# Two-layer macaron transformer on one core: norms, background products and attention look-ahead reordered in both mixers

## The chip, the cores and the metric

One core of a Trainium2 chip. The time is device microseconds of one execution of the whole program; three runs of the kernel before gave a median of 1093.55 us (1093.55 to 1095.39).

## The reference, cut to what matters

The input is one sequence of 256 tokens with 1024 features, in fp32. Two layers each do feed-forward, mixer, feed-forward, all with a modulated norm and a gated residual:

```
mod = (silu(c) @ ada_w[i] + ada_b[i]).reshape(b, 3, 3, d)          # shift, scale, gate for three blocks
y = rms_norm(x, g) * (1 + scale) + shift                           # before each block
x = x + 0.5 * gate * swiglu(y, ffn_w_in, ffn_w_out)                # blocks 0 and 2 of a layer
x = x + gate * mixer(y)                                            # block 1
```

The mixer of layer 0 ("even") projects y to 1720 columns: a low-rank q (256), a low-rank kv (128) and a rope key (32), each of which gets an rms norm, then q, k and v of a sparse attention (nsa). The low-rank parts go through two up-projections to eight heads (mla), with a norm on each head; the nsa part has eight heads with a compressed, a selected and a windowed branch. Both outputs are concatenated and projected back. The mixer of layer 1 ("odd") projects to 3072 columns and has twelve dilated heads in three groups, joined by their softmax denominators, and four moba heads.

## The kernel before, in words

The 256 tokens are two tiles of 128 (t=0 and t=1). fp32 accuracy in the large products comes from splitting both operands into a rounded part H and a rest L (both fp32r) and adding three matmuls (`mm3`, L204 to L206). Weights are split on the fly: `prep` lets ScalarE (ACT) copy a loaded weight piece to H (L167) and VectorE (DVE) take the difference L (L172). A split piece sits in one of four buffers (`hl`), or in one of four more that a stage opens for pieces of its phase (`open_extra`). `piece(i)` hands a piece to a product, `pop` frees it and prepares the next.

All weights come through one list of load jobs, in order, into eight slots of 1 MB (`pump`). A slot is loaded again when its job is done and all jobs ahead of it are done too; SP issues the loads in that order.

The modulation vectors and gates are computed on DVE beside the rest: slices of `ada_w` come through the same slots, and each slice takes two background steps of two products each (L503). `bg(n)` runs up to n steps, but only those whose slice stands in the job list ahead of the next piece to be prepared. The tuples PT, PD, PC, PB, PA (even mixer) and QT to QA (odd mixer) say how many steps each call may run: PT in the tail of feed-forward 0, PD and PC in the t=0 and t=1 loops of the first projection, PB in the second projection, PA in the attention's iterations. Each call is one tick. When a vector is complete its end is put into `fins` with a due tick: for a norm vector a small matmul and three DVE operations (L551 to L559); for a half gate `finA` (ACT copy L580, DVE difference L581) and `finB` (two matmuls L589, ACT copy L590).

The even mixer goes: first projection (columns 0 to 800) of t=0, then of t=1, in eight steps each; second projection (`proj1`) in eight steps of both tiles; norms of the low-rank parts into `cqn` (L1296 to L1307); transposes into cT and T4; q up-projection (L1348), kv up-projection (L1383), compression (L1415); transposes of q and k (`turn`, L1428); the attention in 16 units (eight mla, eight nsa) and 19 iterations. An iteration runs, on PE, the output product of two units (`s3`), transposes of the probabilities (`turns`) and scores of a later unit (`s0`, with dummy matmuls that `keep_warm` adds); on DVE the scaling of the probabilities and the logits of a later unit; on ACT the exponentials (L1062) and copies (L1100); then `fill`, which runs the compressed branch, background steps and the first parts of the output projection (EF, OF). The odd mixer has the same shape with 8 units and 11 iterations, four of them joint over three branches.

Touched are `open_extra`, `prep`, the job order (EVA, EVO), `gate_steps`, `norm_steps` by FBN, the tuples, `bg_flush`, `attention`, `OutProj.end`, `even` and `odd`.

Of the kernel before, what the change touches and what calls it, by code (L numbers as in the profile page):

```python
# [36 lines left out]
def kernel(  # L37
# [89 lines left out]
    def open_extra(pool, n, ph, w=1024):  # L127
        extra.update(pool=pool, n=n, phase=ph, w=w)
# [204 lines left out]
    EVA = ((0, 1), (0, 2), (0, 3), (1, 0), (1, 1))  # L333
    EVC = (((0, 0, 416), (416, 928, 384)), ((0, 416, 512), (512, 1312, 408)))
    ev_ada = list(plan_ada["ev"])
    for h in range(2):
        m = (800, 920)[h]
        phase[0] = ("ev", -1)[h]
        for kh in range(4):
            add_job(("evi", h, kh), [(  # L340
                lambda t, m=m, d=d, n=n: t[:, 0:2 * m].rearrange("p (k c) -> p k c", k=2)[:, :, d:d + n],
                AP(ev_w_in, kh * 256 * 1720 + c, [[1720, 128], [128 * 1720, 2], [1, n]])) for d, c, n in EVC[h]])
            for k in range(2):
                add_piece(("evi", h, kh), lambda t, k=k, m=m: t[:, m * k:m * k + m], ident_dst, 128, m, k == 1)
            if (h, kh) in EVA:
                ada_slot(*ev_ada.pop(0))
# [21 lines left out]
    EVO = ((0, 1), (1, 1))  # L368
# [194 lines left out]
    def gate_steps(n, q):  # L563
        st = []
        i, b = divmod(n, 3)
        s = 6 * b + q

        def begin():
            st.append(small.tile([128, 512], F32, tag="ada", name="ada", bufs=3))
            G.memset(st[0], 0.0)  # L570
            G.dma_start(st[0][0:1, :], AP(ada_b, i * 9 * D + s * 512, [[512, 1], [1, 512]]))

        def part(jh, js):
            products(st[0], slot4(("ada", i, s, jh)), cact[:, 4 * jh:4 * jh + 4], js, False)
# [40 lines left out]
    FBN = 0, 4, 12, 5, 5, 5  # L615
# [3 lines left out]
    OF = {7: ((0, 0),), 8: ((0, 1),), 9: ((0, 2),)}  # L619
    FBG = 5  # L620
# [53 lines left out]
    def bg_flush():  # L674
        while bgq:
            bg_next()
        due(True)
# [344 lines left out]
    def attention(ap, units, stile, lag, fill, warm):  # L1022
# [106 lines left out]
        s0(0)  # L1129
        s0(1)  # L1130
        logits(0)
        for i in range(n + lag + 1):
            if i >= 2 + lag and (i - lag) % 2 == 0:
                s3(i - 1 - lag)
            if lag == 2 and 2 <= i < n + 2:
# [7 lines left out]
            if lag == 1 and 1 <= i <= n:  # L1143
                turns(i - 1)
            if lag == 1 and i + 2 < n:
                s0(i + 2)
            if i < n:
                exps(i)
            s4()
            if lag <= i < n + lag:  # L1150
                out_of(i - lag)
            settle()
            fill(i)

    class OutProj:
# [27 lines left out]
        def end(self):  # L1183
# [3 lines left out]
            for t in range(2):  # L1187
# [5 lines left out]
                for q in range(2):  # L1193
                    for j in range(QM):
# [18 lines left out]
    def even(blk):  # L1213
# [17 lines left out]
        with tc.tile_pool(name="hlev", bufs=4) as ph:  # L1231
            open_extra(ph, 4, ("ev",), 800)
            heads()
            keep_warm(pa[0][0], WKB[0])
            for k in range(8):
# [3 lines left out]
                if k == TRE:  # L1239
                    piece(7)  # L1240
                    blk.tr(1)
            for k in range(8):
                mm(pa, 0, 1, k, *piece(0))
                pop()
                bg(PC[k])
            close_extra()
        with tc.tile_pool(name="ev", bufs=1) as ep:
# [37 lines left out]
            proj1(0, 2)  # L1285

            c32 = ((0, 256, 256), (256, 384, 128), (384, 416, 32))
# [3 lines left out]
            jk = xtile()  # L1291
            ss = small.tile([128, 2, 3], F32, tag="mss", name="mss")
            rr = small.tile([128, 2, 3], F32, tag="mrr", name="mrr")
            for t in range(2):
                for q, (c0, c1, m) in enumerate(c32):
                    A.activation(jk[:, 0:c1 - c0], pa[t][0][:, c0:c1], AF.Square, accum_out=ss[:, t, q:q + 1])  # L1296
# [24 lines left out]
            for t in range(2):  # L1321
# [4 lines left out]
                V.tensor_copy(T4[0:64, :, 128 * t:128 * t + 128], pv[0:64])  # L1326
                if t == 0:
                    V.tensor_copy(T4[64:128, :, 0:127], pv[64:128, :, 1:128])
                else:
                    V.tensor_copy(T4[64:128, :, 127:255], pv[64:128])  # L1330
# [10 lines left out]
            proj1(4, 6)  # L1341
# [35 lines left out]
            proj1(6, 8)  # L1377
# [11 lines left out]
            for t in range(2):  # L1389
                vw = pb[t][1][:, 0:384].rearrange("p (a c) -> p a c", c=128)  # L1390
                V.tensor_copy(kn[t][:, 1], vw[:, 1])
# [32 lines left out]
            def turn(src, dst, sc, t):  # L1424
                for hh in range(2):
                    ps = acc()
                    for j in range(4):
                        T.transpose(ps[0:96, 128 * j:128 * j + 128], src[:, 4 * hh + j, :], ident)  # L1428
                    scaled_evac(dst[:, 4 * hh:4 * hh + 4, 128 * t:128 * t + 128],
                                ps[0:96, :].rearrange("p (h c) -> p h c", h=4), vec[3][0:96, sc:sc + 1])  # L1430
# [19 lines left out]
            V.tensor_copy(hh, ph[:, 0:256])  # L1450
# [5 lines left out]
            with tc.tile_pool(name="ev2", bufs=1) as e2:  # L1456
# [14 lines left out]
                def nsaT(t):  # L1471
# [4 lines left out]
                    scaled_evac(qT[:, :, tsl], ps.rearrange("p (a c) -> p a c", a=4), gq["n"])  # L1476
# [3 lines left out]
                    scaled_evac(kT[:, :, tsl], ps[:, 0:256].rearrange("p (a c) -> p a c", a=2), gk["n"])  # L1480
# [16 lines left out]
                def c1():  # L1497
# [6 lines left out]
                    V.tensor_copy(cc, pc[0:30, 0:128].rearrange("p (v c) -> p v c", v=2))  # L1504
# [50 lines left out]
                def c8():  # L1555
                    V.tensor_copy(PcT, hold["p"][:, 0:256])
# [3 lines left out]
                def fill(i):  # L1560
# [8 lines left out]
                    if i >= 12:  # L1569
# [37 lines left out]
                bg_flush()  # L1607
# [3 lines left out]
    def odd(blk):  # L1611
# [9 lines left out]
        with tc.tile_pool(name="hlod", bufs=4) as ph:  # L1621
            open_extra(ph, 4, ("od",))
# [14 lines left out]
        with tc.tile_pool(name="od", bufs=1) as op_:  # L1637
# [74 lines left out]
            with tc.tile_pool(name="od2", bufs=1) as o2:  # L1712
# [28 lines left out]
                bg_flush()  # L1741
# [249 lines left out]
```

## Time and profile before

| | us |
|---|---|
| median of 3 runs | 1093.55 |
| profiled execution, its own time | 1094.18 |
| its span, first to last instruction | 1092.4 |
| TensorE busy | 1038.4 |
| VectorE busy | 827.3 |
| ScalarE busy | 532.5 |
| mean granted TensorE clock, share of full | 0.989 |

PE is TensorE, DVE VectorE, ACT ScalarE, POOL GpSimd, SP the engine that issues the loads. Starts are microseconds from the span's start. By the timeline the even mixer's first projection starts behind the transposes at 232, its second at 257.5, its attention at 307.5, its output projection ends at 383.7; the odd mixer's first projection starts behind 770, its attention at 846.3, and its output projection ends at 892.9.

### The profile page before, as it was taken

What the parts mean: (1) busy time and instruction counts of PE and PEld (TensorE: products, weight loads), DVE (VectorE), ACT (ScalarE), POOL (GpSimd) and SP (SyncE); (2) the same over time, 40 slices, a digit from 0 to 9 for tenths busy, and PEclk for the clock granted to TensorE, in tenths of its full rate; (3) what the DMA queues carried; (4) which work ended last, traced back from release to release, by engine and by line L of the source; (5) the groups of instructions that cost most, each with busy time, mean ns of one, the idle gap of its engine ahead of it and who ended that gap; (6) DMA issues with size and microseconds to landing.
All of it is one profiled execution on the core that took longest, in us unless ns stands there. A gap on an engine that the chain in (4) does not pass through costs nothing.

```text
span 1092.4 us, 13983 instructions
## 1 busy us (share of the span) xinstructions
PE 1038.4 (95%) x4983; PEld 837.6 (77%) x4983; DVE 827.3 (76%) x1430; ACT 532.5 (49%) x913; POOL 45.9 (4%) x93
## 2 busy tenths in 40 slices
PE   5899999997889989999999999999999899999998
PEld 5578778876676768888887888888688677888886
DVE  5779867769889689988658998854879868566643
ACT  3444433644258675444446544433645756444441
POOL 3000010002500000000000000000000000000000
PEclk9999999999889999999999999999999999999999
DMA  9999998837690448998853999883288517666401
GB/s 334 320 361 332 325 348 233 286 126 234 240 255 15 154 154 296 365 354 271 283 173 123 308 360 340 289 282 117 77 270 232 163 45 263 226 230 201 155 1 39
DMA packets 169818, 250.77 MB, mean 230 GB/s; under 512 B 10741, under 2 KB 111559, under 8 KB 169748
## 3 DMA queue, kind: packets, MB, share of 16 engines
q1 hardware_dynamic: 166736, 248.35, 69.5%
q0 software_dynamic: 2576, 1.39, 0.9%
q8 instruction: 39, 0.64, 0.2%
q14 instruction: 31, 0.25, 0.1%
q10 hardware_dynamic: 436, 0.13, 0.0%
HBM read 247.59 MB, written 2.23 MB: 229 GB/s over the span
## 4 chain that ended last, share of the span: by engine, by line
PE 76%; DVE 13%; ACT 4%; DMA 4%; issue 2%; POOL 0%; SPq 0%; ACTq 0%; DVEq 0%
PE wps L204 12%; PE wps L206 12%; PE wps L205 12%; PE acc L204 11%; PE acc L206 11%; PE acc L205 11%; DVE L L172 3%; DMA slot<-in_ffn_w_in_dram 2%; DVE ada L503 2%; DMA slot<-in_ada_w_dram 1%; ACT xn L1062 1%; ACT H L167 1%; PE wps L888 1%; DVE xn L1049 1%; PE acc L888 1%
## 5 line engine op out<-in xcount | busy, mean ns | idle before, releaser
L172 DVE TENSOR_TENSOR L<-slot,H 128x1024 fp32r<-128x1024 f32 (+4 forms) x316 | 376.4, 1200 | 128.3 <-ACT H L167 123.4
L167 ACT ACTIVATE H<-slot 128x1024 fp32r<-128x1024 f32 (+4 forms) x316 | 325.6, 1040 | 276.0 <-PE wps L206 137.4
L205 PE MATMUL wps<-L,y 128*128 128x512 f32 (+1 forms) x448 | 174.4, 389 | 5.6 <-DVE L L172 4.7
L204 PE MATMUL wps<-H,y 128*128 128x512 f32 (+1 forms) x448 | 177.3, 396 | 1.7 <-ACT y L1835 1.6
L206 PE MATMUL wps<-H,y 128*128 128x512 f32 (+1 forms) x448 | 173.7, 388 | 0.0
L204 PE MATMUL acc<-H,y 128*128 128x512 f32 (+2 forms) x416 | 162.5, 391 | 3.5 <-ACT y L722 1.6
L205 PE MATMUL acc<-L,y 128*128 128x512 f32 (+2 forms) x416 | 159.6, 384 | 4.0 <-DVE L L172 4.0
L206 PE MATMUL acc<-H,y 128*128 128x512 f32 (+2 forms) x416 | 159.7, 384 | 0.1
L503 DVE SCALAR_TENSOR_TENSOR ada<-slot,c,ada 128x512 f32<-128x512 f32 x155 | 116.2, 750 | 2.9
L205 PEld LDWEIGHTS wps<-L,y 128*128 128x128 f32 x448 | 84.9, 190 | 25.0 <-DVE L L172 9.6
L204 PEld LDWEIGHTS wps<-H,y 128*128 128x128 f32 x448 | 84.9, 190 | 19.4 <-ACT y L1835 2.0
L206 PEld LDWEIGHTS wps<-H,y 128*128 128x128 f32 x448 | 84.7, 189 | 17.4 <-DVE y L728 0.4
L205 PEld LDWEIGHTS acc<-L,y 128*128 128x128 f32 x416 | 78.2, 188 | 19.4 <-DVE L L172 5.9
L204 PEld LDWEIGHTS acc<-H,y 128*128 128x128 f32 x416 | 78.2, 188 | 18.2 <-ACT y L722 1.8
L206 PEld LDWEIGHTS acc<-H,y 128*128 128x128 f32 x416 | 78.1, 188 | 15.7 <-DVE y L728 0.9
L503 DVE SCALAR_TENSOR_TENSOR ada<-slot,cact,ada 128x512 f32<-128x512 f32 x96 | 72.1, 751 | 5.5 <-DMA slot<-in_ada_w_dram 3.6
L204 PE MATMUL acc<-H,gT 128*128 128x512 f32 (+1 forms) x176 | 71.3, 405 | 1.0 <-DVE g L876 1.0
L204 PE MATMUL wps<-H,gT 128*128 128x512 f32 (+1 forms) x176 | 71.2, 404 | 0.0
L206 PE MATMUL acc<-H,gT 128*128 128x512 f32 (+1 forms) x176 | 69.3, 394 | 0.0
L205 PE MATMUL acc<-L,gT 128*128 128x512 f32 (+1 forms) x176 | 69.2, 393 | 0.0
L206 PE MATMUL wps<-H,gT 128*128 128x512 f32 (+1 forms) x176 | 69.1, 393 | 0.0
L205 PE MATMUL wps<-L,gT 128*128 128x512 f32 (+1 forms) x176 | 69.0, 392 | 0.0
(352 smaller groups left out, 1230.9 us busy)
## 6 DMA issues: line engine op xcount, KB each, us to landing
slot<-in_ffn_w_in_dram SPq DMA_DIRECT2D x160, 512.0 KB, 6.7
slot<-in_ffn_w_out_dram SPq DMA_DIRECT2D x40, 1024.0 KB, 7.5
slot<-in_ada_w_dram SPq DMA_DIRECT2D x160, 256.0 KB, 5.6
slot<-in_ada_w_dram SPq DMA_DIRECT2D x24, 1024.0 KB, 8.2
slot<-in_od_w_in_dram SPq DMA_DIRECT2D x12, 1024.0 KB, 5.3
slot<-in_ada_w_dram SPq DMA_DIRECT2D x16, 512.0 KB, 9.5
slot<-in_ffn_w_in_dram SPq DMA_DIRECT2D x16, 384.0 KB, 4.3
slot<-in_nsa_cmp_w_dram SPq DMA_DIRECT2D x4, 1024.0 KB, 9.0
```

The lines of the kernel that those rows point to most:

```text
L167: A.activation(hv, w, AF.Copy)
L172: eng.tensor_tensor(lv, w, hv.bitcast(F32), op=OP.subtract)
L204: T.matmul(o, lhsT=sh, rhs=wh, start=start, stop=False)
L205: T.matmul(o, lhsT=sh, rhs=wl, start=False, stop=False)
L206: T.matmul(o, lhsT=sl, rhs=wh, start=False, stop=stop)
L503: V.scalar_tensor_tensor(a, w[:, j], c[:, j:j + 1], a, op0=OP.mult, op1=OP.add)
L888: T.transpose(ps[0:mm, 256 * ft + 128 * t:256 * ft + 128 * t + 128], st[u, t][:, 128 * ft:128 * ft + mm], ident)
L1049: V.tensor_tensor_reduce(out=s[b][:, 128:384], in0=ps[:, 128:384], in1=M[:, 0:256], scale=-1.0, scalar=3e38, op0=OP.add, op1=OP.min, accum ...
L1062: A.activation(s[b][:, c0:c1], s[b][:, c0:c1], AF.Exp, scale=-1.0, bias=nm[:, b, q:q + 1], accum_out=den[:, b, q:q + 1])
```

## The change

The load order of the even mixer puts two modulation slices ahead of the first projection's weights, one behind the sixth and one behind the eighth of its loads, and the four gate slices two and two around the output weights. `prep` fills the four common buffers first and the extra ones after them in the mixers. A half gate's `finB` is put on the list only when `finA` has run, three ticks later. The tuples have new quotas. At the end of the attention `bg_end` runs what is left but only one end; `OutProj.end` runs the others ahead of the second half of the first tile's last products. `attention` issues scores three units and logits two units ahead of the iteration (two and one before). In the even mixer the squares of tile 0 are taken inside the t=1 loop, the norms of the low-rank parts are issued ahead of the second projection, whose eight steps now stand 2, 1, 2, 3 between the norms, the transposes, the q and the kv up-projection (they stood 2, 2, 2, 2); and some fifteen copies and scalings out of PSUM go to ScalarE in place of VectorE.

```diff
-        if extra["live"] < extra["n"] and ph in extra["phase"]:
+        if npre[0] >= cap[0]:
+            return False
+        here = extra["live"] < extra["n"] and ph in extra["phase"]
+        if len(ready) - extra["live"] < HLN and not (here and not extra["last"]):
+            pool = hl
+        elif here:
             pool = extra["pool"]
             extra["live"] += 1
-        elif len(ready) - extra["live"] < HLN:
-            pool = hl
...
-    EVA = ((0, 1), (0, 2), (0, 3), (1, 0), (1, 1))
+    EVA = ((1, 1), (1, 3))
     ev_ada = list(plan_ada["ev"])
+    for _ in range(2):
+        ada_slot(*ev_ada.pop(0))
...
-    for a in ev_ada:
-        ada_slot(*a)
     for j in range(4):
+        if j % 2 == 0:
+            for _ in range(2):
+                ada_slot(*ev_ada.pop(0))
         add_job(("evo", j), [(
...
-    EVO = ((0, 1), (1, 1))
+    EVO = ((0, 1), (1, 1), (2, 1), (3, 1))
...
             owed.append(lambda: V.tensor_tensor(st[2], st[0], st[1].bitcast(F32), op=OP.subtract))
+            fins.insert(0, (tick[0] + FBG, finB))
...
-            [(2, finA), (FBG, finB)]
+            [(2, finA)]
...
-    FBN = 0, 4, 12, 5, 5, 5
+    FBN = 0, 4, 5, 5, 5, 5
-    OF = {7: ((0, 0),), 8: ((0, 1),), 9: ((0, 2),)}
-    FBG = 5
+    OF = {6: ((0, 0),), 7: ((0, 1),), 9: ((0, 2),)}
+    FBG = 3
+    AH = 2
-    PA = 1, 1, 0, 1, 0, 1, 1, 1, 1, 1, 1, 1, 1, 1, 1, 1, 1, 2, 1, 0
-    PT = 2, 1, 0, 1, 0, 0, 0, 0
+    PA = 1, 1, 0, 1, 0, 0, 0, 0, 0, 0, 0, 0, 0, 0, 0, 1, 1, 1, 1, 0
+    PT = 0, 0, 1, 1, 0, 0, 0, 0
-    PC = 1, 1, 1, 1, 2, 1, 1, 1
-    PB = 1, 1, 1, 2, 1, 1, 0, 0
+    PC = 0, 1, 0, 1, 0, 1, 1, 0
+    PB = 1, 1, 0, 0, 0, 0, 1, 0
-    QC = 0, 0, 0, 0, 0, 0, 0, 0
+    QC = 0, 1, 0, 1, 0, 0, 0, 0
...
-    def bg_flush():
+    def bg_end():
         while bgq:
             bg_next()
-        due(True)
+        if fins:
+            fins.pop(0)[1]()
...
-        s0(0)
-        s0(1)
-        logits(0)
+        for i in range(AH):
+            s0(i)
+            if i == 0:
+                continue
+            logits(i - 1)
+        s0(AH)
+        logits(AH - 1)
         for i in range(n + lag + 1):
...
-            if lag == 2 and i + 2 < n:
-                s0(i + 2)
+            if i + AH + 1 < n:
+                s0(i + AH + 1)
             if 1 <= i <= n:
                 scale(i - 1)
-            if i + 1 < n:
-                logits(i + 1)
+            if i + AH < n:
+                logits(i + AH)
...
                 for q in range(2):
+                    if q:
+                        due(True)
...
+            cap[0] = npre[0] + 16
...
+                if k == 3:
+                    for q, (c0, c1, m) in enumerate(c32):
+                        A.activation(jk[:, 0:c1 - c0], pa[0][0][:, c0:c1], AF.Square, accum_out=ss[:, 0, q:q + 1])
...
-            proj1(0, 2)
...
-                V.tensor_copy(kn[t][:, 0], pa[t][1][:, 256:384])
+                A.activation(kn[t][:, 0], pa[t][1][:, 256:384], AF.Copy)
                 for q, (c0, c1, _) in enumerate(c32):
-                    V.tensor_scalar(cqn[t][:, c0:c1], pa[t][0][:, c0:c1], rr[:, t, q:q + 1], None, op0=OP.mult)
+                    if t:
+                        A.activation(cqn[t][:, c0:c1], pa[t][0][:, c0:c1], AF.Copy, scale=rr[:, t, q:q + 1])
+                    else:
+                        V.tensor_scalar(cqn[t][:, c0:c1], pa[t][0][:, c0:c1], rr[:, t, q:q + 1], None, op0=OP.mult)
...
+            proj1(0, 2)
             bank[0] = acc
-            proj1(2, 4)
+            proj1(2, 3)
...
-            proj1(4, 6)
+            proj1(3, 5)
...
-            proj1(6, 8)
+            proj1(5, 8)
...
+                    if (t, hh) == (0, 1):
+                        V.tensor_scalar(dst4, src4, g, None, op0=OP.mult)
+                    else:
+                        A.activation(dst4, src4, AF.Identity, scale=g)
...
+                    if i == 11:
+                        cap[0] = 1 << 30
-                    if i >= 12:
+                    if i >= 11:
                         prep(True)
```

## Rows read from the trace of the kernel before

**Rows 1.** The page's first part: busy us, share of the span, instructions.

```profile
PE 1038.4 (95%) x4983; PEld 837.6 (77%) x4983; DVE 827.3 (76%) x1430; ACT 532.5 (49%) x913; POOL 45.9 (4%) x93
```

**Rows 2.** Waits of PE by line: releaser; us in total, times, longest.

```profile
PE acc L1318 <- DVE cqn L1307: 6.5, 2, 6.0
...
PE wps L589 <- DVE ahl L581: 3.0, 1, 3.0
...
PE wps L1090 <- ACT PT L1100: 2.6, 1, 2.6
...
PE acc L1383 <- issue: 1.3, 1, 1.3
...
PE acc L1415 <- POOL qf L1281: 0.9, 1, 0.9
```

**Rows 3.** Windows: stretch, busy us (instructions) by engine, PE clock, DMA share, GB/s.

```profile
270.00:280.00 10.00, 5.85 (x23) 5.19 (x24) 6.81 (x23) 0.95 (x2) 4.51 (x11) 0.66 1.08 360
...
280.00:290.00 10.00, 9.90 (x40) 7.01 (x39) 9.00 (x13) 1.97 (x4) 3.00 (x4) 1.00 0.54 188
...
310.00:320.00 10.00, 6.64 (x38) 5.77 (x37) 9.39 (x36) 4.38 (x16) 2.07 (x4) 0.83 1.09 327
...
320.00:330.00 10.00, 9.35 (x62) 7.73 (x60) 7.01 (x31) 6.06 (x22) 0.00 (x0) 0.83 0.96 202
...
330.00:340.00 10.00, 10.00 (x74) 7.06 (x74) 9.54 (x45) 7.16 (x26) 0.00 (x0) 1.00 0.01 4
...
380.00:390.00 10.00, 7.37 (x35) 5.38 (x34) 7.52 (x17) 8.75 (x14) 0.00 (x0) 1.00 0.00 0
```

**Rows 4.** Timeline of PE: start us, us, engine, line, tile; idle before it.

```profile
273.69 0.45 PE L1318 MATMUL acc<-cp,cqn 128*128 128x128 f32 x1 [6.00 <-DVE cqn L1307]
...
277.29 0.78 PE L204 MATMUL wps<-H,y 128*128 128x512 f32 x1
...
279.45 0.39 PE L204 MATMUL wps<-H,y 128*128 128x512 f32 x1
```

**Rows 5.** Timeline of DVE in the same stretch.

```profile
259.56 6.49 DVE L503 SCALAR_TENSOR_TENSOR ada<-slot,c,ada 128x512 f32<-128x512 f32 x8
...
265.97 3.11 DVE L503 SCALAR_TENSOR_TENSOR ada<-slot,cact,ada 128x512 f32<-128x512 f32 x4
...
271.05 0.30 DVE L488 TENSOR_SCALAR mss<-mss 128x2 f32<-128x2 f32 x3
...
274.07 0.89 DVE L1307 TENSOR_SCALAR cqn<-acc,mrr 128x256 f32<-128x256 f32 x3
```

**Rows 6.** Timeline of DVE and PE in the first attention iterations.

```profile
316.39 0.68 DVE L581 TENSOR_TENSOR ahl<-ada,ahl 128x512 fp32r<-128x512 f32 x1
...
318.78 1.06 PE L1036 MATMUL wps<-yb,yb 96*128 96x256 f32 x2
...
323.54 0.60 PE L1036 MATMUL wps<-yb,yb 96*128 96x256 f32 x2
```

**Rows 7.** Timeline of DVE and PE around the even attention's end.

```profile
363.58 3.49 DVE L172 TENSOR_TENSOR L<-slot,H 128x1024 fp32r<-128x1024 f32 x3
...
371.88 0.42 DVE L841 TENSOR_TENSOR yb<-acc,yb 128x256 fp32r<-128x256 f32 x1 [4.81 <-ACT yb L840]
...
372.22 1.22 DVE L172 TENSOR_TENSOR L<-slot,H 128x1024 fp32r<-128x1024 f32 x1
...
372.61 0.39 PE L206 MATMUL wps<-H,oT 128*128 128x512 f32 x1
```

**Rows 8.** Timeline of ACT and PE in the odd attention.

```profile
856.75 0.40 ACT L1062 ACTIVATE xn<-xn,nj 128x128 f32<-128x128 f32 x1 [2.57 <-DVE nj L1053]
...
873.68 0.90 PE L1090 MATMUL wps<-cp,xn 128*128 128x128 f32 x3 [2.56 <-ACT PT L1100]
...
874.23 0.78 PE L204 MATMUL acc<-H,oTo 128*128 128x512 f32 x1
```

**Rows 9.** Timeline of SP's DMA queue behind the even projections.

```profile
304.66 9.60 SPq L101 DMA_DIRECT2D slot<-in_ffn_w_in_dram  x6
```

More of the change, by code (lines that the diff above doesn't have):

```diff
@@ L125, in add_piece, with open_extra @@
         pieces.append((name, src, dst, rows, cols, last, phase[0]))
-    def open_extra(pool, n, ph, w=1024):
-        extra.update(pool=pool, n=n, phase=ph, w=w)
+    cap = [1 << 30]
+    def open_extra(pool, n, ph, w=1024, last=False):
+        extra.update(pool=pool, n=n, phase=ph, w=w, last=last)
     def close_extra():
@@ L1134, in attention @@
                 s3(i - 1 - lag)
-            if lag == 2 and 2 <= i < n + 2:
+            if 2 <= i < n + 2:
                 turns(i - 2)
-            if lag == 2 and i + 2 < n:
-                s0(i + 2)
+            if i + AH + 1 < n:
+                s0(i + AH + 1)
             if 1 <= i <= n:
                 scale(i - 1)
-            if i + 1 < n:
-                logits(i + 1)
[L1143 to L1146, printed above, removed]
+            if i + AH < n:
+                logits(i + AH)
             if i < n:
@@ L1231, in even @@
         with tc.tile_pool(name="hlev", bufs=4) as ph:
-            open_extra(ph, 4, ("ev",), 800)
+            open_extra(ph, 4, ("ev",), 800, True)
+            cap[0] = npre[0] + 16
             heads()
@@ L1241, in even @@
                     blk.tr(1)
+            jk = xtile()
+            ss = small.tile([128, 2, 3], F32, tag="mss", name="mss")
+            c32 = ((0, 256, 256), (256, 384, 128), (384, 416, 32))
             for k in range(8):
@@ L1284, in even @@
             bank[0] = None
-            proj1(0, 2)
-            c32 = ((0, 256, 256), (256, 384, 128), (384, 416, 32))
             cqn = [e1.tile([128, 416], F32, name=f"cqn{t}") for t in range(2)]
@@ L1290, in even @@
             qn = ep.tile([128, 2, 4, 2, 64], F32, name="qn")
-            jk = xtile()
-            ss = small.tile([128, 2, 3], F32, tag="mss", name="mss")
             rr = small.tile([128, 2, 3], F32, tag="mrr", name="mrr")
-            for t in range(2):
-                for q, (c0, c1, m) in enumerate(c32):
-                    A.activation(jk[:, 0:c1 - c0], pa[t][0][:, c0:c1], AF.Square, accum_out=ss[:, t, q:q + 1])
+            for q, (c0, c1, m) in enumerate(c32):
+                A.activation(jk[:, 0:c1 - c0], pa[1][0][:, c0:c1], AF.Square, accum_out=ss[:, 1, q:q + 1])
             kcd = xtile()[:, 0:1024].rearrange("p (t a b c) -> p t a b c", t=2, a=4, b=2)
@@ L1325, in even @@
                 pv = ps.rearrange("p (a c) -> p a c", a=4)
-                V.tensor_copy(T4[0:64, :, 128 * t:128 * t + 128], pv[0:64])
+                A.activation(T4[0:64, :, 128 * t:128 * t + 128], pv[0:64], AF.Copy)
                 if t == 0:
-                    V.tensor_copy(T4[64:128, :, 0:127], pv[64:128, :, 1:128])
+                    A.activation(T4[64:128, :, 0:127], pv[64:128, :, 1:128], AF.Copy)
                 else:
-                    V.tensor_copy(T4[64:128, :, 127:255], pv[64:128])
+                    A.activation(T4[64:128, :, 127:255], pv[64:128], AF.Copy)
             AA = xtile()[:, 0:1024].rearrange("p (v i a) -> p v i a", v=2, i=16)
@@ L1390, in even @@
                 vw = pb[t][1][:, 0:384].rearrange("p (a c) -> p a c", c=128)
-                V.tensor_copy(kn[t][:, 1], vw[:, 1])
+                A.activation(kn[t][:, 1], vw[:, 1], AF.Copy)
                 jk = xtile()[:, 0:768]
@@ L1428, in turn @@
                         T.transpose(ps[0:96, 128 * j:128 * j + 128], src[:, 4 * hh + j, :], ident)
-                    scaled_evac(dst[:, 4 * hh:4 * hh + 4, 128 * t:128 * t + 128],
-                                ps[0:96, :].rearrange("p (h c) -> p h c", h=4), vec[3][0:96, sc:sc + 1])
+                    src4, dst4 = ps[0:96, :].rearrange("p (h c) -> p h c", h=4), dst[:, 4 * hh:4 * hh + 4, 128 * t:128 * t + 128]
+                    g = vec[3][0:96, sc:sc + 1]
+                    if (t, hh) == (0, 1):
+                        V.tensor_scalar(dst4, src4, g, None, op0=OP.mult)
+                    else:
+                        A.activation(dst4, src4, AF.Identity, scale=g)
             kf = []
@@ L1449, in even @@
             hh = PcT
-            V.tensor_copy(hh, ph[:, 0:256])
+            A.activation(hh, ph[:, 0:256], AF.Copy)
             V.tensor_scalar(gt, gt, 1.0, None, op0=OP.add)
@@ L1475, in nsaT @@
                         T.transpose(ps[:, 128 * p:128 * p + 128], qn[:, t, p].rearrange("q g c -> q (g c)"), ident)
-                    scaled_evac(qT[:, :, tsl], ps.rearrange("p (a c) -> p a c", a=4), gq["n"])
+                    A.activation(qT[:, :, tsl], ps.rearrange("p (a c) -> p a c", a=4), AF.Identity, scale=gq["n"])
                     ps = acc()
@@ L1479, in nsaT @@
                         T.transpose(ps[:, 128 * b:128 * b + 128], kn[t][:, b], ident)
-                    scaled_evac(kT[:, :, tsl], ps[:, 0:256].rearrange("p (a c) -> p a c", a=2), gk["n"])
+                    A.activation(kT[:, :, tsl], ps[:, 0:256].rearrange("p (a c) -> p a c", a=2), AF.Identity, scale=gk["n"])
                 def fold():
@@ L1503, in c1 @@
                                      start=k == 0, stop=k == 1)
-                    V.tensor_copy(cc, pc[0:30, 0:128].rearrange("p (v c) -> p v c", v=2))
+                    A.activation(cc, pc[0:30, 0:128].rearrange("p (v c) -> p v c", v=2), AF.Copy)
                     A.activation(kcn[:, 0], cc[:, 0], AF.Square, accum_out=sk)
@@ L1555, in c8 @@
                 def c8():
-                    V.tensor_copy(PcT, hold["p"][:, 0:256])
+                    A.activation(PcT, hold["p"][:, 0:256], AF.Copy)
                 chain = [c0, c1, c2, c3, c4, c5, c6, c7, c8]
@@ L1606, in even @@
                 attention(e2, units + [mk2(p, b) for p in range(4) for b in range(2)], ring, 2, fill, WKE)
-                bg_flush()
+                bg_end()
                 return proj_out.end()
@@ L1621, in odd @@
         with tc.tile_pool(name="hlod", bufs=4) as ph:
-            open_extra(ph, 4, ("od",))
+            open_extra(ph, 4, ("od",), 1024, True)
             heads()
@@ L1740, in odd @@
                 attention(o2, units, ring, 2, fill, WKO)
-                bg_flush()
+                bg_end()
             return proj_out.end()
```

## The prediction

> **What bounds the kernel now.** Start with the busy shares [rows 1]: TensorE (PE) is busy 1038.4 of 1092.4 us. No edit removes matmuls, so all that can be won is the 54 us in which PE stands, and the time it runs at the lower clock. The waits of PE come next [rows 2]: five of the longest lie in the two mixers. 6.5 us is the transposes of the normed latents waiting for VectorE (DVE, L1307); 3.0 is a gate matmul behind L581; 2.6 is a transpose behind ScalarE's copy L1100; 1.3 and 0.9 are L1383 and L1415. The rest are block seams and feed-forward stages the diff leaves alone. The windows [rows 3] show what such a wait costs beside itself: in 270 to 280 us the granted clock averages 0.66 (of its two levels, 2.4 and 1.2 GHz, the lower for about two thirds of the stretch), while ScalarE has 0.95 us of work and DVE 6.81.
>
> Why does PE wait at 267.7? Read the two engines side by side [rows 4, 5]. PE has finished four of the eight steps of the second projection and needs cqn. DVE executes in order and has twelve modulation products ahead of the norm: eight from 259.56 to 265.97 and four to 268.99. The mean starts at 271.05, cqn follows at 273.07 and 274.07. So the norm is late because of what stands ahead of it on DVE, not for want of data.
>
> Durations below come from the profiled execution, 1094.18 us (span 1092.4 and 1.78 around it). The median shown, 1093.55, is 0.63 below; I take that off at the end.
>
> **The change part by part.** A background step is two products, 1.5 us of DVE (four products take 3.11) [rows 5]. The second set of modulation vectors takes eight steps, the gate of the first mixer's output eight.
>
> *Steps that move.* A step runs only where its call has a quota and its slice stands ahead of the next weight piece in the load queue. Walking the new order through that rule: the first two slices are now ahead of the first projection, so two steps run in the tail of feed-forward 0 and one at the end of the t=0 loop; the t=1 loop runs three, at k=1, 3 and 5; the quotas at k=6 and at steps 0 and 1 of the second projection find a slice that still stands behind unprepared pieces, so nothing; one runs at step 6. That is seven. Three follow in the first four attention iterations, one each in iterations 15 to 18, two in the flush behind. In the old order ten ran up to the norm, four later in the projection, two in the attention. So seven steps, 10 us of DVE, leave the stretch ahead of the norm, and six land at the attention's end.
>
> *Norms ahead of the second projection.* Three of six squares run inside the t=1 loop. With DVE free by about 257.5, the norm chain (3.8 us by the rows from 271.05 to the end of cqn at 274.9) plus some 2.2 us of squares and copies on ScalarE ends near 263, while PE does three projection steps, 2.5 us each by its four in 10.1 us, until 265.1. I cost the norm at nothing: these three steps hide it, with some 2 us to spare. This takes away the 6.00 and 0.47 us of waiting and the lower clock behind it: from 273.69 to 279.45 fourteen transposes and six matmuls take about 2.2 us more than at the full clock (0.78 us for the 512-column matmul at 277.29, 0.39 at 279.45) [rows 4]. Together 8.7 us.
>
> *Three projection steps behind the q up-projection instead of two.* They give DVE 7.5 us for the q norm, which took 5 us plus the 1.3 us that L1383 waited [rows 2]: 1.3 goes. Of the 0.9 at L1415 I take half, as it may rest on ScalarE's copies of v as well. The price: six of eight evacuations of qf and kf now queue on ScalarE, so that the first scores come about 0.5 us later. The other copies moved there, of 0.3 to 0.7 us, meet an engine with 1.97 us of work in 280 to 290 [rows 3], where DVE has 9.00: nothing. An ACT version of these scalings is not in the trace; bounds: 0.1 us saved each, as the ScalarE twins of L836 are slightly shorter, to 1 us lost in all if they queue. Front of the even mixer: 8.7+1.3+0.5-0.5 = 10.0 us; bounds 6, if one of these waits moves to a copy, and 11.
>
> *Gate in two steps.* The gate's end (copy to fp32r on ScalarE, difference on DVE, matmul) was run in one go in iteration 0; PE reached the matmul and waited 3.04 us for L581, queued behind an hT chain, and then ran below the clock (L1036 x2 1.06 us at 318.78, 0.60 at 323.54) [rows 6]. Now the matmul follows three calls later, and here it leaves the place altogether. But DVE is nearly the bound there: in the three windows from 310 to 340 it idles 4.06 us [rows 3]; three steps instead of two add 1.5, while two evacuations and two small copies sent to ScalarE (2.2, an estimate by the sizes of L581) and two differences that leave (1.36) take off 3.5. Of the 6 us that PE loses I therefore take 2.6; bounds 0 and 6. Scores and logits two units ahead help DVE use the idle time; their order adds no instruction. In the nsa units the score tiles are a ring of nine for ten now live: one write waits for the transposes of the same iteration, which PE has already queued. Nothing, as PE is busy without a gap there; bound 2 us lost.
>
> *The end of the even attention.* Here the change adds a wait. In iteration 18 DVE waits until 371.88 for the last output (L841), having idled since 367.07, then splits a piece (L172, 1.22) [rows 7]. The new order queues behind: step 14 of 16, the first gate difference (0.68, L581 in [rows 6]), steps 15 and 16, another split, the second difference. The first gate matmul stands in PE's queue right behind the product that ends near 372.8; its difference is ready at 371.9+0.3+1.1+1.5+0.6 = 375.4: PE waits 2.6 us, with all of the output projection queued behind. As behind the wait in the odd mixer [rows 8], I add 1.4 for the lower clock. The four gate matmuls themselves, 0.25 each, now stand where PE is the bound: 1.0; the second difference, 0.3. Sum 5.3 lost; bounds 0, if DVE reaches it in time, and 7, if two more splits stand ahead.
>
> [...] The granted clock in 380 to 390 stays at 1.00 though PE is busy only 7.37 us [rows 3], and behind the wait of 2.56 a 512-column matmul takes 0.78 [rows 8]. [...]
>
> *Odd mixer.* ScalarE waits for DVE's logits ahead of every joint exponential (2.57 us at 856.75) while DVE does the scaling and a background step of the unit before; that is what delays L1100 and makes PE wait 2.56 us at 873.68 with slow matmuls behind, to 876.5 [rows 8]. Two units ahead, the logits are there, and all eight background steps of this mixer now run in the projections, where the earlier preparation of two pieces frees DVE 2.5 us. From that wait and 1.4 of clock, 4.0 in all and some small waits beside, I take 3.7, since scaling of a joint unit must still wait for the logits ahead of it on DVE; bounds -1 and 5.
>
> Other moved items at nothing: the cap and the pool order change where pieces lie, not how many; DMA issues on SP are the same number, two slices earlier; the gate's bias load and memset on POOL follow their steps. Sum: -10.0-2.6+5.3-3.7 = -11.0; 1094.18-11.0-0.63 = 1082.6 us.
>
> **Rivals.** (a) No pile-up at the end: the last steps slip into DVE's idle 4.81 us [rows 7] and the early attention gives its 6. Against it: DVE is in order and step 14 is issued behind L841. 5.3-1.0+3.4 = 7.7 better: 1075. (b) A wait takes the place of the one removed: cT or T4 waits for ScalarE, whose queue now has squares, copies and splits ahead, or the early attention stays bound by DVE. Half of the front lost and nothing in the attention: 5+2.6 worse: 1090. For it: DVE was at 9.00 in 280 to 290. Against: ScalarE is nearly idle there. (c) Slower: the eight load slots are freed in order, and slices of the gate now sit in them until iterations 16, 18 and the flush. Feed-forward 1 had three double loads issued from 304.66 [rows 9]; now one is in before iteration 16. Price: six slices of 1 MB at the 360 GB/s of [rows 3] are 2.8 us each, 16.8 us of debt; if none of it hides, 1082.6+16.8 = 1099. It decides when more than four of the six (11 us) fall on PE; against it speaks that DMA moves nothing in 380 to 390 [rows 3], and that the next loads are not wanted before about 390. (d) Everything cancels: 1093.5.
>
> **How the numbers follow.** Forecast 1082.6 (own range 1079 to 1087) 0.56; (a) 0.14; (b) 0.18; (d) 0.04; (c) 0.08. Leaving out the lower half of (a), (d) and (c), about 0.19, the range is 1075.5 to 1090.5. About 0.2% (2.2 us) is what measurements of this kernel can tell: faster 0.88, within 0.04, slower 0.08.
>
> **What would show it.** Right: no wait of PE on cqn, granted clock 1.00 between 265 and 290, attention starting some 10 us earlier; no wait of about 3 us at the first gate matmul in iteration 0, but one of 2 to 3 us at L589 just ahead of the output projection; in the odd mixer joint exponentials back to back and no wait near 2.5 us on L1100. Wrong: a wait of several us at cT, at L1383 or at the first matmuls of feed-forward 1 for slots; or an unchanged length of the odd attention.

## The result, and the profile after

The changed kernel takes 1082.46 us (median of 4, 1079.88 to 1083.83) against 1094.47 for the kernel before on the same chip (4 runs, 1093.55 to 1095.66): a ratio of 0.9887, 95% interval 0.9865 to 0.9909. The forecast was 1082.6. The profiled execution of the changed kernel is its fastest, 1079.88 us, with a span of 1078.1 from the first instruction to the last, 14.3 under the span before. So the parts below add up to 14.3, not to the 12.0 between the medians.

The page of the changed kernel, first part: busy us, share of the span, instructions (as [rows 1]).

```profile
PE 1035.7 (96%) x4983; PEld 835.0 (77%) x4983; DVE 819.0 (76%) x1412; ACT 539.7 (50%) x931; POOL 43.5 (4%) x93
```

PE's busy time is 2.7 us less for the same 4983 instructions; the rest of the 14.3 us is time in which it stood. Its waits by line (as [rows 2]: releaser; us in total, times, longest; the old L1318 is L1339, L589 is L599, L1090 is L1103):

```profile
PE acc L599 <- DVE ahl L590: 2.3, 1, 2.3
PE acc L1103 <- DVE xn L1094: 1.8, 2, 1.2
...
PE acc L1726 <- ACT qTo L847: 1.2, 1, 1.2
PE acc L1133 <- ACT PT L1113: 1.2, 1, 1.2
...
PE acc L1345 <- ACT cT L847: 0.3, 1, 0.3
```

All five waits of [rows 2] are gone from their places. The largest new one, 2.3 us, is the gate matmul's, now at the even attention's end. Windows of the changed kernel (columns as [rows 3]):

```profile
270.00:280.00 10.00, 10.00 (x41) 7.38 (x40) 4.80 (x15) 1.96 (x4) 2.59 (x5) 1.00 0.31 106
310.00:320.00 10.00, 9.33 (x67) 6.69 (x66) 8.74 (x45) 4.15 (x16) 1.01 (x2) 0.83 1.05 304
360.00:370.00 10.00, 10.00 (x38) 8.10 (x37) 7.03 (x12) 3.45 (x8) 0.49 (x1) 0.84 0.88 311
370.00:380.00 10.00, 7.78 (x31) 5.46 (x30) 8.25 (x17) 8.75 (x13) 0.00 (x0) 0.85 0.03 5
380.00:390.00 10.00, 9.31 (x37) 7.28 (x36) 9.62 (x19) 4.29 (x8) 0.00 (x0) 0.81 0.87 295
```

From 270 to 280 PE is busy throughout at the full clock, where it had 5.85 us at 0.66. Behind the new wait, in 360 to 370, the granted clock is low. It is low again from 370 to 390, behind the first waits of the next block; that costs nothing, as the stage lengths below the table show. The front in DVE's and PE's timelines (as [rows 4, 5]):

```profile
255.87 3.21 DVE L512 SCALAR_TENSOR_TENSOR ada<-slot,c,ada 128x512 f32<-128x512 f32 x4
259.00 0.40 DVE L497 TENSOR_SCALAR mss<-mss 128x2 f32<-128x2 f32 x3
...
261.12 0.90 DVE L1327 TENSOR_SCALAR cqn<-acc,mrr 128x256 f32<-128x256 f32 x3
...
264.15 0.82 PE L1339 MATMUL acc<-cp,cqn 128*128 128x128 f32 x6
```

Four products stand just ahead of the norm, not twelve; cqn is done at 262.0, 2.1 us before PE comes to it. The even attention's end (as [rows 7]):

```profile
357.19 1.53 DVE L512 SCALAR_TENSOR_TENSOR ada<-slot,cact,ada 128x512 f32<-128x512 f32 x2
358.63 0.68 DVE L590 TENSOR_TENSOR ahl<-ada,ahl 128x512 fp32r<-128x512 f32 x1
359.23 3.11 DVE L512 SCALAR_TENSOR_TENSOR ada<-slot,cact,ada 128x512 f32<-128x512 f32 x4
...
359.37 0.50 PE L599 MATMUL acc<-ahl,onesr 128*128 128x512 f32 x1 [2.31 <-DVE ahl L590]
...
360.44 0.63 PE L212 MATMUL wps<-H,yb 128*128 128x512 f32 x1
```

To place the time, take the starts of the same rows in PE's timeline of each profiled execution and subtract. A: the even mixer's first transposes to its first scores; B: on to the first product with the compressed values (VB); C: on to the last of these; D: on to the next block's transposes; E: the odd mixer's second transposes to its first scores; F: on to the start of its last output product with v; G: on to the next transposes. In the kernel before, for instance, F and G part here:

```profile
883.16 2.17 PE L1120 MATMUL wps<-PT,vt 128*64 128x256 f32 x16
...
892.90 1.04 PE L703 MATMUL wps<-cp,xn 128*128 128x128 f32 x8
```

| kernel | A | B | C | D | E | F | G |
|---|---|---|---|---|---|---|---|
| before | 75.75 | 39.02 | 22.83 | 14.35 | 63.24 | 36.87 | 9.74 |
| after | 64.27 | 35.23 | 22.81 | 19.55 | 64.37 | 32.30 | 9.74 |
| norm behind (e1) | 66.58 | 35.23 | 22.84 | 18.19 | 64.31 | 32.16 | 9.74 |
| products ahead (e2) | 76.45 | 36.37 | 23.31 | 14.34 | 64.30 | 32.29 | 9.74 |
| gate early (e3) | 64.26 | 35.23 | 24.18 | 15.31 | 64.31 | 32.32 | 9.74 |
| one ahead (e4) | 64.29 | 34.10 | 23.83 | 18.19 | 65.87 | 34.42 | 9.75 |
| odd steps back (e5) | 64.42 | 35.22 | 22.82 | 19.51 | 63.31 | 32.12 | 9.73 |
| gate one go (e6) | 76.63 | 36.37 | 23.29 | 14.35 | 64.33 | 32.17 | 9.74 |
| copies on DVE (e7) | 64.34 | 37.97 | 22.70 | 18.17 | 64.33 | 32.55 | 9.73 |
| steps in idle (e8) | 64.27 | 34.50 | 24.16 | 15.31 | 64.34 | 32.51 | 9.74 |
| norm end late (e9) | 75.34 | 37.11 | 23.30 | 14.34 | 64.34 | 32.40 | 9.74 |
| gate early, odd steps back (e10) | 64.28 | 35.24 | 24.17 | 15.30 | 64.80 | 32.12 | 9.74 |
| all three (e11) | 64.26 | 34.56 | 23.70 | 15.30 | 63.30 | 32.12 | 9.74 |

After minus before: A -11.48, B -3.79, C -0.02, D +5.20, E +1.13, F -4.57, G 0. From D's end to E's start both take some 399.3 us, though the clock is low from 370 to 390 in the changed kernel alone. Another -0.88 lies ahead of the first mixer: its transposes start anywhere from 228.9 to 233.5 us in these profiles, and what sets that was not tested. What is left is 0.1.

### The profile page after: what moved, and what is told of

Read it like the earlier page. It is cut to its first block, busy times and chain, and to the rows that moved or that the text cites. A ratio compares the mean times of both kernels' runs of the same rounds, so it can differ in the third digit from the quotient of the medians.

```text
span 1078.1 us, 13969 instructions
## 1 busy us (share of the span) xinstructions
PE 1035.7 (96%) x4983; PEld 835.0 (77%) x4983; DVE 819.0 (76%) x1412; ACT 539.7 (50%) x931; POOL 43.5 (4%) x93
## 4 chain that ended last, share of the span: by engine, by line
PE 81%; DVE 9%; DMA 4%; ACT 3%; issue 1%; SPq 1%; ACTq 0%; DVEq 0%
PE wps L210 12%; PE wps L212 12%; PE wps L211 12%; PE acc L210 12%; PE acc L212 12%; PE acc L211 12%; DVE L L178 3%; DMA slot<-in_ada_w_dram 2%; DMA slot<-in_ffn_w_in_dram 1%; ACT H L173 1%; SPq L101 1%; PE wps L901 1%; PE acc L901 1%; DMA yb<-scr 1%; PE wps L1133 1%
## 5 line engine op out<-in xcount | busy, mean ns | idle before, releaser
L210 PE MATMUL acc<-H,y 128*128 128x512 f32 (+2 forms) x416 | 164.2, 395 | 4.0 <-ACT y L735 1.6
L212 PE MATMUL acc<-H,y 128*128 128x512 f32 (+2 forms) x416 | 161.6, 388 | 0.1
```

Source lines behind the costliest of these rows:

```text
L210: T.matmul(o, lhsT=sh, rhs=wh, start=start, stop=False)
L212: T.matmul(o, lhsT=sl, rhs=wh, start=False, stop=stop)
```

## The experiments

The kernel before took 1094.37 us beside e1 to e4, 1095.23 beside e5 to e8 and 1094.57 beside e9 to e11. Executions of one kernel scatter by up to 6 us, so the table above, in which stages that an edit leaves alone mostly repeat to 0.2 us, tells more than a median where the edit is small.

**e1: the norm behind two projection steps again.**

```
+            proj1(0, 2)
             cqn = [e1.tile(...) ...]     # squares, mean, scaling
             ...
-            proj1(0, 2)
             bank[0] = acc
```

> The changed kernel with one thing undone: the squares, the mean and the scaling of the latents stand behind steps 0 and 1 of the second projection again, and the moved modulation products stay where the change put them. In the changed kernel cqn is ready at 262.0 us and PE wants it at 264.15, so 2.1 us are spare. Theory A (both halves of the edit were needed): the two splits of steps 0 and 1 stand ahead of the squares on ScalarE, and the second can only start when PE frees its buffer, about 261.7; squares to 263.7, mean and scaling 3 us, cqn at 266.7: PE waits 2.5 us at the latents' transposes and pays some 1.5 us of lower clock behind: 4 us slower, about 1086.5. Rival (the products alone were the cause): the spare time hides the two steps, no wait, 1082.5. Rival (the place alone was the cause): the wait of 6.5 us is back with 2.2 us of clock: 1091.

1084.16 us (ratio 0.9904, 0.9887 to 0.9921). PE's waits show the one that theory A had:

```profile
PE acc L1339 <- DVE cqn L1328: 2.2, 1, 2.2
```

A grows by 2.31 us, the wait alone: the granted clock stays at 1.00 behind it, so theory A's 1.5 us of clock did not come. The norm's place is worth 2.3 us while the products are out of the way. The rivals fall.

**e2: the modulation products ahead of the norm again.**

```
-    EVA = ((1, 1), (1, 3))          # two slices also ahead of the first
+    EVA = ((0, 1), (0, 2), (0, 3), (1, 0), (1, 1))
-    PC = 0, 1, 0, 1, 0, 1, 1, 0     # PT, PB, PA likewise
+    PC = 1, 1, 1, 1, 2, 1, 1, 1
```

> The changed kernel with the old order of the modulation slices in the load queue and the old quotas of the even mixer: some ten steps run ahead of the norm again and two in the attention; the norm keeps its new place. Theory A: at the front DVE gets to the norm at about 265 us, cqn at 268, PE wants it at 264.2: a wait of about 4 us and 2 us of clock, 6 us lost; at the attention's end the wait of 2.3 us on the first gate difference, the lower clock behind it and the late steps go, 5.3 us won: about 1083, the same as the change. Rival (where the norm stands was the cause of the front's gain): nothing lost at the front, 5.3 won at the end: 1077. Rival (the end's 5.3 was not the steps' doing but the seam's): 6 lost, nothing won: 1088.5.

1090.36 us (0.9966, 0.9955 to 0.9978), 7.9 slower than the change. D is 14.34, so the 5.2 us at the end are the late steps' doing, as theory A had it. The front lost twice what it expected, 12.2 us. PE's waits from 255 to 310, three rows of its timeline and two windows:

```profile
PE acc L1336 <- DVE cqn L1324: 4.4, 1, 4.4
PE acc L1342 <- ACT cT L844: 1.7, 1, 1.7
PE acc L1433 <- POOL ada L576: 1.6, 1, 1.6
PE acc L557 <- DVE ada L509: 1.0, 1, 1.0
```

```profile
265.19 1.03 PE L557 MATMUL acc<-cp,ada 128*128 128x4 f32 x8 [1.02 <-DVE ada L509]
...
270.63 1.51 PE L1336 MATMUL acc<-cp,cqn 128*128 128x128 f32 x6 [4.42 <-DVE cqn L1324]
...
294.18 3.60 PE L1401 MATMUL acc<-slot,cT 128*128 128x512 f32 x8
```

```profile
260.00:270.00 10.00, 5.19 (x29) 4.40 (x27) 9.30 (x23) 0.08 (x1) 3.55 (x9) 0.87 1.07 367
270.00:280.00 10.00, 7.68 (x31) 6.75 (x32) 5.04 (x10) 7.26 (x13) 6.83 (x16) 0.62 0.95 314
```

By the starts of the cqn transposes (264.15 in the changed kernel, 270.63 here), 6.6 of the 12.2 come ahead of them: waits of 4.4 and 1.0 us, and the matmuls at L557 themselves, 1.0, which the changed kernel runs in B. The other 5.6 come behind: waits of 1.7 and 1.6 us, and the lower clock (0.62 in 270 to 280). The kv up-projection (L1401), which waited 1.3 us in the kernel before, doesn't wait here.

**e3: two gate steps earlier in the even attention.**

```
-    PA = 1, 1, 0, 1, 0, 0, 0, 0, 0, 0, 0, 0, 0, 0, 0, 1, 1, 1, 1, 0
+    PA = 1, 1, 0, 1, 0, 0, 0, 0, 0, 0, 0, 0, 0, 1, 1, 1, 1, 1, 1, 0
```

> The changed kernel with two quotas more: steps 11 and 12 of the first gate run in attention iterations 13 and 14, so that the last four steps run in 15 to 18 and none is left for the flush. Theory A (the end's price is DVE's queue: 2.3 us of wait, the lower clock of three windows behind it, the relocated matmuls): the first difference is done two iterations earlier, DVE's idle 2.42 us ahead of the last output takes a step in, the wait goes, clock 1.00 from 360 to 400: 4 us won, about 1078.5, with the second difference still in the flush. Rival (DVE at 9.76 of 10 us in 340 to 350 is the bound): the steps delay the outputs by the 3 us they take, and nothing is won: 1082.5 or slower. Rival (the lower clock comes from the block seam): only the wait goes, 2.3 won: 1080.

1078.58 us (0.9855, 0.9840 to 0.9870), the time that theory A had. PE no longer waits at the gate matmul, and the clock stays up behind it:

```profile
350.00:360.00 10.00, 10.00 (x57) 7.77 (x57) 9.56 (x18) 4.82 (x8) 1.01 (x2) 1.00 0.82 265
360.00:370.00 10.00, 10.00 (x46) 8.25 (x45) 7.47 (x17) 5.37 (x10) 0.00 (x0) 1.00 0.84 301
```

It still falls at the next block's start (0.76 in 370 to 380), against theory A's 1.00 up to 400, and again at no cost (399.3 us from D's end to E's start). D falls by 4.24; C, where the two steps now run, grows by 1.37, the share of the first rival. So the trace shows 2.9 us, less than the 3.9 between the medians and theory A's 4. The 0.96 by which D stays above the kernel before are the four gate matmuls.

**e4: scores and logits one unit ahead.**

```
-    AH = 2
+    AH = 1
```

> The changed kernel with scores and logits one unit ahead, as before the change, in both attentions. Theory A (looking two units ahead is what removed ScalarE's waits ahead of the joint exponentials): in the odd attention the wait near 2.5 us on the copy of the transposed probabilities is back with its slow matmuls, 4 us lost; in the even attention 0 to 2 us lost: about 1087. Rival (the eight background steps that left the odd attention did it): the odd attention stays as it is, 1082.5. Rival (the even attention's early part gained its 3.8 us by the look-ahead): another 3.8 lost, 1090.

1082.84 us (0.9891, 0.9873 to 0.9909), not theory A's 1087: no difference that the medians can tell. The trace can. ScalarE's idle times ahead of the four joint exponentials of the odd attention are back, by its timeline:

```profile
842.37 0.40 ACT L1075 ACTIVATE xn<-xn,nj 128x128 f32<-128x128 f32 x1 [0.90 <-DVE nj L1066]
848.55 0.40 ACT L1075 ACTIVATE xn<-xn,nj 128x128 f32<-128x128 f32 x1 [2.57 <-DVE nj L1066]
854.80 0.40 ACT L1075 ACTIVATE xn<-xn,nj 128x128 f32<-128x128 f32 x1 [1.51 <-DVE rd L1090]
862.05 0.40 ACT L1075 ACTIVATE xn<-xn,nj 128x128 f32<-128x128 f32 x1 [2.25 <-DVE nj L1066]
```

The 2.57 is that of [rows 8] to the digit; in the changed kernel only 0.91 and 0.93 are left of the four. F is 2.12 longer, half of what theory A expected. In the even attention two units ahead only trade B (+1.13) for C (-1.02).

**e5: the odd mixer's background steps back among its attention's units.**

```
-    EVO = ((0, 1), (1, 1), (2, 1), (3, 1))      -    QC = 0, 1, 0, 1, 0, 0, 0, 0
+    EVO = ((0, 1), (1, 1))                      +    QC = 0, 0, 0, 0, 0, 0, 0, 0
```

> The changed kernel with the odd mixer's gate slices where they stood before and no steps in the t=1 loop of its projections; the look-ahead of two stays. The background steps run among the odd attention's units again. In the run with scores one unit ahead the odd attention took 34.4 us from its first scores to its last output, against 32.3 in the changed kernel and 37.5 before, so some 3 us should belong to the steps. Theory A: 3 us lost in the odd attention, 1.1 won back in the projections ahead of it: 1084.4. Rival (with two units ahead the steps are covered): the attention keeps 32.3, the projections give 1.1 back: 1081.4.

1080.14 us (0.9878, 0.9859 to 0.9896). F stays at 32.12 and E gives 1.06 back: the rival. Either edit alone shortens F (36.87 to 34.42 with the steps out and one unit ahead, to 32.12 with the steps in and two ahead), and with two ahead the steps' move only costs. (The expectation's 37.5 for the kernel before is 36.9 when F ends where that product starts, as in the other kernels.)

**e6: e2 with the gate's end in one go.**

```
-            fins.insert(0, (tick[0] + FBG, finB))     # in finA
-            [(2, finA)]
+            [(2, finA), (FBG, finB)]                  # FBG = 5
```

> The kernel of the run with the modulation products ahead of the norm again (1090.4), and in it the gate's end in one go as before: copy, difference and matmul in the same call. Theory A (the split in two steps is what removed the wait of 3.04 us in attention iteration 0): the wait is back with slow matmuls behind it, 3.5 us more from the first scores to the first output of the second kind (36.4 to about 39.9): 1094. Rival (the early attention is bound by DVE and the wait only stood for that): no more than 1 us longer: 1091.

1091.30 us (0.9968, 0.9955 to 0.9980), B 36.37 as in e2. The split in two steps is worth nothing, in this kernel with the vectors' end due after 5 calls.

**e7: the evacuations back on DVE.**

```
-                A.activation(T4[0:64, ...], pv[0:64], AF.Copy)       # and kn, cqn, cc, PcT, hh
+                V.tensor_copy(T4[0:64, ...], pv[0:64])
-                    A.activation(qT[:, :, tsl], ..., AF.Identity, scale=gq["n"])   # kT, qf, kf
+                    scaled_evac(qT[:, :, tsl], ..., gq["n"])
```

> The changed kernel with all evacuations that moved to ScalarE back on DVE (cqn, kn, T4, half of qf and kf, half of qT and kT, cc, PcT, hh). Theory A (they move work between two engines that both have room at the front; DVE idles 8 us between 266 and 277): the front keeps its 64.3 us from first transposes to first scores to within 1 us, the early attention, where DVE has 9.4 to 9.8 of 10 us, loses 1 to 2: about 1084. Rival (DVE's relief by the copies was a good part of the front's gain): 4 us or more lost ahead of the first scores: 1087 or more. Rival (the copies queue on ScalarE and cost): faster by 0.5 to 1: 1081.5.

1084.16 us (0.9910, 0.9896 to 0.9924). A is the same to 0.1 us; B is 2.74 longer, and PE waits longer for the scaled probabilities (`xn`) from DVE. Two of PE's waits, 1.8 and 1.2 us in the changed kernel:

```profile
PE acc L1103 <- DVE xn L1094: 3.5, 3, 1.3
...
PE acc L1133 <- ACT PT L1113: 3.0, 3, 1.5
```

**e8: e3, and two steps in DVE's idle time of the second projection.**

```
-    PA = 1, 1, 0, 1, 0, ...        -    PB = 1, 1, 0, 0, 0, 0, 1, 0      -  cap[0] = npre[0] + 16
+    PA = 1, 0, 0, 0, 0, ...        +    PB = 1, 1, 0, 1, 1, 0, 1, 0      +  cap[0] = npre[0] + 12
```

> The version with the gate's steps 11 and 12 in iterations 13 and 14 (1078.6), and two of the three steps of the first attention iterations moved into steps 3 and 4 of the second projection, where DVE idles 8 us between 266 and 277. Theory A (DVE bounds the early attention): 3 us of DVE leave it, of which PE, whose waits there are 1.8 and 1.2 us with a granted clock of 0.83 in one window, gets 1.5 to 3 back: about 1076.5. Rival (the early attention is bound by the order of ScalarE's exponentials, 10.0 us busy in 330 to 340): nothing, 1078.6. Rival (the two steps delay the q norm, which starts at 274.4 as soon as ScalarE has its squares): slower, 1080.

1078.84 us (0.9855, 0.9840 to 0.9870), no gain over e3 by the medians, and not theory A's 1076.5. B is 0.73 shorter: of the 3 us taken off DVE a quarter reaches PE. A stays, so the steps don't hold up the q norm. Whether ScalarE, busy all of 330 to 340 here (10.00), takes the other three quarters was not tested.

**e9: e6 with the second modulation vectors' end due late.**

```
-    FBN = 0, 4, 5, 5, 5, 5
+    FBN = 0, 4, 12, 5, 5, 5
```

> The kernel of the run with the gate's end in one go (1091.3), and in it the end of the second modulation vectors due 12 background calls after their last product, as before, instead of 5. The ends stand in one queue and run in its order, so the gate's copy and difference wait behind it for attention iteration 0. Theory A (that place in the queue, and not the one go, made the wait of 3.04 us): the gate matmul of iteration 0 waits about 3 us for its difference behind the hT chain, and from first scores to the first output of the second kind it takes 39 to 40 us instead of 36.4: about 1093.5, less some 1 us for the matmuls that leave the front. Rival (the wait was DVE's load by the evacuations since moved): no wait over 1 us, 36.4 as before: 1091.

1089.72 us (0.9961, 0.9948 to 0.9973). PE's timeline has the wait of [rows 2] back, and what follows it at the low clock:

```profile
317.38 0.51 PE L595 MATMUL wps<-ahl,onesr 128*128 128x512 f32 x1 [2.71 <-DVE ahl L587]
...
318.47 1.06 PE L1045 MATMUL wps<-yb,yb 96*128 96x256 f32 x2
```

So the place of the ends in their queue made that wait. But B grows by 0.74 only, while A falls by 1.29, as the vectors' matmuls, 0.95 us, move from A into B. Without the late end, in e6, PE waits elsewhere in this stretch, and e9 has neither of these waits:

```profile
PE acc L1099 <- DVE xn L1090: 1.2, 1, 1.2
...
PE acc L1523 <- ACT PT L1109: 0.7, 1, 0.7
```

The clock differs as well (0.73 in 320 to 330 in e6, 0.93 in e9), so what the wait costs by itself is not shown.

**e10 and e11: what won, put together.** e10 is e3 with e5, e11 is e8 with e5.

> Two edits that each won, in one kernel: the gate's steps 11 and 12 in attention iterations 13 and 14 (1078.6, 3.9 under the changed kernel), and the odd mixer's steps back among its attention's units (1.25 us shorter from second transposes to the next stage in that run's trace). They lie in different mixers: if they add, 1077.3. If the odd edit's 1.25 was a chance of that execution: 1078.6.

> The same two edits and the two steps in DVE's idle time of the second projection, which shortened the even mixer by 0.7 us in its trace, while its median did not move: if the trace counts, 1076.6; if not, as the run beside it, 1077.3.

e10 takes 1076.84 us (1075.51 to 1081.67; ratio 0.9848, 0.9826 to 0.9870), e11 1074.06 us (1074.01 to 1079.30; 0.9832, 0.9811 to 0.9853): e11 is the fastest kernel here, 8.4 us under the change by the medians, with the two-unit look-ahead and the moved norm kept. By the table 5.3 of them lie in A to G; the rest is less than the scatter. e10's E of 64.80 has a low clock at its start (0.86 in 760 to 770); in e5 and e11, with the same steps, E is 63.3. DVE's idle time at the front is partly filled, 8.05 us busy (4.80 in the changed kernel):

```profile
270.00:280.00 10.00, 10.00 (x42) 7.68 (x41) 8.05 (x25) 1.96 (x4) 4.30 (x8) 1.00 0.91 312
```

## Why the prediction was right

**The front: forecast -10.0 (6 to 11), measured -11.5.** The mechanism was the right one: norm late by what stands ahead of it on DVE, hidden by three projection steps with some 2 us to spare (2.1). The waits and the clock that the prediction priced, 6.47, 2.2, 1.3 and 0.9, make 10.9; it was too careful in taking half of the last and 0.5 us for later first scores, which did not come. One sentence of it miscounts: by its own list ten steps ahead of the norm become six, so four leave that stretch and not seven; the other three leave the projection behind the norm. e1 and e2 split the gain: products ahead of the norm cost 12.2 us, the norm's old place 2.3. Of e2's loss 5.6 us lie behind cqn's arrival, from its transposes to the first scores (31.0 us in the changed kernel, 36.6 in e2). They are the lower clock, a wait for ScalarE's cT and one ahead of the compression, and not the 1.3 at the kv up-projection, which doesn't wait in e2. With the copies undone A stays too (e7), so the 1.3 probably went with the third step ahead of it, which no run undid.

**The early attention: forecast -2.6 (0 to 6), measured -3.8; the step that failed is "gate in two steps".** The split does nothing (e6). The wait of 3.04 us came from the order of the ends: the norm's, due 12 calls after its last product, held back the gate's, and the change sets 5; the prediction did not weigh that number. Nor was it worth what it took: with it back (e9) B is only 0.7 longer, and A 1.3 shorter, since without it PE waits for DVE and ScalarE nearby (e6). The low clock that the prediction priced with it costs nothing here in the changed kernel: B is 35.23 us with 0.83 in 310 to 320, and 35.23 in e1 with 1.00. Most of the gain is the copies that moved to ScalarE, 2.7 (e7); the prediction had those of the attention, as 2.2 us in DVE's balance, but took its gain from the time that PE loses there. Products back ahead of the norm cost B another 1.1 (e2); the look-ahead moves 1.1 us from C to B and gains nothing here. These parts overlap and don't add up to 3.8.

**The attention's end: forecast +5.3 (0 to 7), measured +5.2.** Wait 2.31 for 2.6, its clock 1.4 for 1.4 (D is 19.5 where the clock fell behind it, in the changed kernel and e5, and 18.2 in e1, e4 and e7, where it did not), four matmuls 0.96 for 1.0; 0.6 is left where the second difference had 0.3. That the clock fell behind this wait, as forecast, is partly luck: in three kernels of five it did not. e2 and e3 show that the pile-up could be avoided, so this half of rival (a) was a matter of two quotas, though e3 pays 1.4 of the 4.2 us back in C.

**The odd mixer: forecast -3.7 (-1 to 5), measured -3.4.** ScalarE's waits for DVE's logits went with the look-ahead (e4, e5): F -4.6. The forecast missed that the steps moved into the projections cost there, E +1.1 (half of it in PE's wait at L1726 for ScalarE's copy, 1.2 us against 0.6 in e5 and before), and counted their leaving the attention as part of the gain; with two units ahead they were covered where they stood (e5).

**The rest.** Rival (b), half of the front lost again, is out. Rival (c), starved slots, is out too: the list has no wait of PE on a weight slot behind the even mixer, and from D to E the two kernels differ by less than 0.1 us. The sum, -11.0, is 3.3 us short of the profiled 14.3, 0.9 of it ahead of the mixers, and 0.1 off the median: so close a hit is partly chance, since executions of one kernel scatter by more and the front and the early attention gained 2.7 us more than forecast.

## What to carry to other kernels

Before moving work away from an engine's queue, look at what stands there twice: at the place it leaves, and at the place where its quota lets it run. Here a gain at the front was given back by a third at the end (5.2 of 15.3 us in the even mixer), and moving two quotas got 2.9 of it back. Price a wait by the bound around it, the engine that the others wait for, and not by its length: putting a wait of 2.7 us back cost 0.7 where PE waits for DVE and ScalarE anyway, 2.3 us were worth 2.3 to 3.7 where PE was the bound. Two cures for one stall don't add: test each alone and drop the one that costs.

## What the runs showed of the hardware

The granted clock behind one and the same wait is not the same from kernel to kernel. The gate matmul at the even attention's end waits 2.31 or 2.32 us in five of these kernels, behind and ahead of the same matmuls. In the changed kernel and in e5 the clock falls (0.84 and 0.83 in 360 to 370), in e1, e4 and e7 it stays at 1.00 there. The first two have the same even mixer, so these are not five independent tries. e4:

```profile
360.00:370.00 10.00, 9.16 (x39) 7.26 (x40) 8.38 (x14) 3.43 (x8) 1.01 (x2) 1.00 0.77 272
...
770.00:780.00 10.00, 8.63 (x36) 7.01 (x35) 5.79 (x13) 4.68 (x8) 0.00 (x0) 0.83 0.62 211
```

The same kernel has 0.83 where the odd mixer begins, behind a wait of 1.4 us, where the changed kernel, with the same wait and as busy (8.63), has 1.00; its E is 1.5 us longer. Where PE is the bound, each such fall costs 1.3 to 1.5 us here. Where it isn't, a fall cost nothing here: e1 has the full clock in the early attention, the changed kernel 0.83 in 310 to 320, and B is 35.23 us in both; e1:

```profile
310.00:320.00 10.00, 9.34 (x78) 7.42 (x78) 8.57 (x42) 5.36 (x20) 1.01 (x2) 1.00 1.05 374
```

How much of the scatter between executions of one kernel such falls make is not shown, since each kernel left one trace. The Trainium skill, "TensorE: Matmul & The Clock Gate", section "HAM oscillation — how this bites in real kernels", tells of a kernel in which each wait for loads, of about 3 to 5 us, starts the next burst cold. Here two of five waits of 2.3 us did, and the wait of 1.4 us in e4. By these rows the prediction's term of 1.4 us was neither certain nor free.
